# Shifting the SBUF addresses of a decoder trunk's matmul operands by 64 bytes, and ten more matmuls on zeros at the start

## The chip, the core and the metric

The kernel runs on one core of a Trainium2 chip. A core has TensorE (matrix products; PE in the profile, with its weight loads shown as PEld), VectorE (DVE), ScalarE (ACT), GpSimd (POOL) and SyncE (SP), which issues the DMA transfers. The engines work at the same time and wait for each other by semaphores. SBUF is the on-chip memory of 128 partitions from which TensorE reads both its operands; PSUM takes its results. The metric is the device time of one execution in microseconds.

## The reference

The computation is a decoder trunk of two layers on 256 tokens of width 1024, in float32. What matters of it:

```python
for l in range(DEPTH):                         # DEPTH = 2
    h = _rmsnorm(x, mix_norm[l])
    proj = h @ w_in[l]                         # 1024 -> 5892 columns
    ret_c, fox_c, rwkv_c, gate_c = split(proj)
    y_ret, y_fox, y_rwkv = retention(ret_c), forgetting_attention(fox_c), rwkv7(rwkv_c)
    merged = sum(gate_b * (y_b @ p_b[l]) for the three branches b)
    x = x + merged @ w_out[l]
    h = _rmsnorm(x, ffn_norm[l])
    g, u = split(h @ w_gate_up[l])             # 1024 -> 2 x 2816
    x = x + (silu(g) * u) @ w_down[l]          # 2816 -> 1024
return x
```

## The kernel before

**Products in three parts.** Activations lie transposed: 128 channels on the partitions, 256 tokens along the row. Float32 precision is kept by splitting each operand into a rounded high part and the low rest, and by forming three products for each block of 128 x 128 weights (`mm3`, L281 to L289): high weights by high activations (L285), high weights by low activations (L288), low weights by high activations (L289). A weight block is the stationary operand, which a load puts into the array, and the 256 columns of an activation part are the streamed operand. Products whose result has the tokens on the partitions (`mm3n`, L429 to L434) swap the roles: the activation part is loaded and 256, 260 or 512 columns of a weight part are streamed.

**Weights in pieces.** `weights()` lists all weights in the order of use, in transfers of 1 MB or less into one of three buffers (`raw`). `_piece` (L251 to L270) takes eight blocks of 128 columns from such a buffer: ScalarE rounds them into a tile `whi` (L268), VectorE subtracts and writes the rest into a tile `wlo` (L269). There are four buffers of each, in turn, and `refill` makes pieces up to three ahead of their use. One piece of eight blocks gives TensorE 24 matmuls of `mm3`. A pair of result blocks over 1024 channels takes two pieces (`gemm_pair`, L291), over 2816 channels five and a half.

**Stages of a layer.** (1) The mixers: products with the input weights, whose streamed operands are the tiles `xh` and `xl` made by `norm_add` (L379); among them, in an order that a table of paces (`PACE`) sets, the three branches with their many small matmuls; then twelve products of the branches' outputs (`hi`, `lo` in the pool `t2`), merged with the gates, and four output products (`hi`, `lo` in `t2` again). (2) The feed-forward part (`ffn`, L571): 22 pairs of gate and up products on `xh`, `xl`, and four pairs of down products on the hidden parts `hh`, `hl` (named `hi`, `lo` in the profile, in the pool `hp`). After the third pair, `replicate` (L421) spreads the norm's factors by one float32 matmul (L424). Within the feed-forward part, TensorE has nothing else to do than `mm3`.

**Where the tiles lie.** Pools are laid one after the other in SBUF, the tags of a pool in order of first use, and a pool that is opened inside a `with` takes the room behind those that are open. `cp`, `raw`, `spl` (the parts of the weights), `xp` (activations) are open throughout; `big`, `t2` and `sm` in the mixers; `hp` and `ft` in the feed-forward part. The addresses of the built program, per partition:

| tiles | address of the first, bytes | step from buffer to buffer | modulo 128 |
|---|---|---|---|
| `whi`, four buffers | 46784 | 4160 (1040 columns of 4 bytes) | 64, 0, 64, 0 |
| `wlo`, four buffers | 63424 | 4160 | 64, 0, 64, 0 |
| `xh` and `xl`, four each | 92352, 100544 | 2048 | 64 |
| `hh`, `hl` (feed-forward) | 113408 | 2048 | 0 |
| `hi`, `lo` of the branches and of the merge | 193376 | 2048 | 96 |

A block is 512 bytes and a half of an activation tile 1024, so the modulus holds within a tile. The two parts of a piece always lie in buffers of the same modulus. The buffers are taken in falling order of address: 0, 64, 0, 64 modulo 128.

**The start.** `__init__` (L152) clears a tile `zero` and runs 20 matmuls on it (L169, L170) into a PSUM tile that nobody reads, and issues the first transfers. Order and waits between engines are made by a planner from the program's order, the paces and priorities. `early` (L243) raises the priority of some work.

Of the kernel before, what the change touches and what calls it, by code (L numbers as in the profile page):

```python
# [8 lines left out]
F32 = mybir.dt.float32  # L9
F32R = mybir.dt.float32r  # L10
# [6 lines left out]
P = 128  # L17
# [133 lines left out]
class Kernel:  # L151
    def __init__(self, ctx, tc, d, depth=DEPTH, debug=None):  # L152
        self.tc, self.nc, self.d, self.depth = tc, tc.nc, d, depth
        self.debug = debug or {}
        nc = self.nc
        e = ctx.enter_context
        self.cp = e(tc.tile_pool(name="cp", bufs=1))
        self.raw = e(tc.tile_pool(name="raw", bufs=3))
        self.spl = e(tc.tile_pool(name="spl", bufs=4))
        self.xp = e(tc.tile_pool(name="xp", bufs=4))  # L160
        self.ps = e(tc.tile_pool(name="ps", bufs=4, space=bass.MemoryType.PSUM))
        self.dr = e(tc.tile_pool(name="dr", bufs=1, space=bass.MemoryType.DRAM))
        self.uid = 0


        zero = self.cp.tile([P, T], mybir.dt.bfloat16, name="zero")
        nc.vector.memset(zero, 0.0)
        pz = self.ps.tile([P, T], F32, tag="fr", bufs=2, name="pz")
        for _ in range(20):  # L169
            nc.tensor.matmul(pz, zero[:, 0:P], zero, start=True, stop=True)  # L170
        par = [self.cp.tile([P, P_RES], F32, name=f"par{l}") for l in range(depth)]
        self.xt = [self.xp.tile([P, 2, T], F32, tag="x", bufs=5, name=f"x0_{j}") for j in range(4)]
        nc.sync.dma_start(self.xt[0], d["xt"][:, 0:2, :])
        nc.sync.dma_start(par[0], d["par"][0, :, 0:P_RES])
        self.jobs, self.raws, self.ready, self.cur = list(self.weights()), [], [], []
        w0 = self.raw.tile([P, 2080], F32, tag="raw", name=self.nm("raw"))
        for j in range(4):
            if j:
                nc.sync.dma_start(self.xt[j], d["xt"][:, 2 * j:2 * j + 2, :])
            if j < 2:  # L180
                nc.sync.dma_start(w0[:, 1024 * j:1024 * (j + 1)], d["win"][0, 0, :, 1024 * j:1024 * (j + 1)])
        self.jobs[0:1] = [(w0, 4, P, 0), (w0, 4, P, 4), (w0, 8, P, 8)]
        self.par = par
        self.con = con = self.cp.tile([P, C_RES], F32, name="con")
        self.identb, self.maskb = zero[:, 0:P], zero[:, P:]
        self.c = {}
        for k, (o, n) in C_OFF.items():
            if k in FETCHED:
                continue
            v = con[:, o:o + n]  # L190
            if k in C_SHAPE:
                v = v.rearrange("p (a b) -> p a b", a=C_SHAPE[k][0])
            self.c[k] = v
        cc = self.c["cc"]
        self.cc = lambda i: cc[:, i:i + 1]

    def load_rest(self):
        self.nc.sync.dma_start(self.con, self.d["const"][:, 0:C_RES])
        self.nc.gpsimd.tensor_copy(self.identb, self.c["ident"])
        self.nc.gpsimd.tensor_copy(self.maskb, self.c["foxmask"])  # L200
        for l in range(1, self.depth):
            self.nc.sync.dma_start(self.par[l], self.d["par"][l, :, 0:P_RES])
# [48 lines left out]
    def _piece(self):  # L251

        nc = self.nc
        if not self.raws:
            src, n, width, o = self.jobs.pop(0)
            if hasattr(src, "shape") and src.shape[-1] == n * width:
                raw = self.raw.tile([P, 2080], F32, tag="raw", name=self.nm("raw"))
                nc.sync.dma_start(raw[:, :n * width], src)
            else:
                raw = src  # L260
            per = min(8, 1040 // width)
            for s in range(0, n, per):
                self.raws.append((raw, o + s, min(per, n - s), width))
        raw, s, m, width = self.raws.pop(0)
        r = raw[:, s * width:(s + m) * width]
        hi = self.spl.tile([P, 1040], F32R, tag="whi", name=self.nm("whi"))
        lo = self.spl.tile([P, 1040], F32R, tag="wlo", name=self.nm("wlo"))
        nc.scalar.copy(hi[:, :m * width], r)  # L268
        nc.vector.tensor_tensor(out=lo[:, :m * width], in0=r, in1=hi[:, :m * width].bitcast(F32), op=ALU.subtract)  # L269
        self.ready.append([(hi[:, i * width:(i + 1) * width], lo[:, i * width:(i + 1) * width]) for i in range(m)])  # L270
# [187 lines left out]
    def layer(self, l):  # L458
        tc, nc, d = self.tc, self.nc, self.d
        if l == 0:  # L460
            self.norm_start(0, "mixg")
            for j in range(4):
                self.norm_add(j, False)
                if j != 2:
                    self.piece()
        xs = self.xs
        with ExitStack() as st:
            e = st.enter_context
            self.big = e(tc.tile_pool(name="big", bufs=1))
            self.t2 = e(tc.tile_pool(name="t2", bufs=13))  # L470
            self.sm = e(tc.tile_pool(name="sm", bufs=1))
            self.mixers(l, xs)
            mx = self.mx

            self.norm_start(l, "ffng")
            for j in range(4):
                if j == 0:
                    ps = self.gemm_halves(mx, 4)
                elif j == 3:
                    ps = self.gemm_halves(mx)  # L480
                else:
                    ps = self.run(self.gemm_pair(mx))
                x = self.xp.tile([P, 2, T], F32, tag="x", bufs=5, name=self.nm("x"))
                for o, p in self.parts(ps):
                    nc.vector.scalar_tensor_tensor(out=x[:, o, :], in0=p, scalar=0.5, in1=self.xt[j][:, o, :], op0=ALU.mult, op1=ALU.add)
                self.xt[j] = x
                self.norm_add(j)
        self.ffn(l)
# [82 lines left out]
    def ffn(self, l):  # L571
# [3 lines left out]
        with ExitStack() as st:  # L575
            e = st.enter_context
            hp = e(tc.tile_pool(name="hp", bufs=1))
            ft = e(tc.tile_pool(name="ft", bufs=3))
            for j in range(FT // 2):
                if j == 0:  # L580
                    pg = self.gemm_halves(xs, 7, tag="rw")
                    _, dg = self.rstd()
# [11 lines left out]
                hi, lo = self.split(hp, h, [P, 2, T], (f"hh{j}", f"hl{j}"))  # L594
# [595 lines left out]
```

## Time and profile before

| | |
|---|---|
| time, median of 3 runs | 813.24 us (812.84 to 814.67) |
| the profiled execution: its own time | 813.39 us |
| its span, first to last instruction | 811.5 us |
| mean granted TensorE clock | 0.995 |
| PE busy, share of the span | 797.3 us, 98% |
| DVE, ACT, POOL busy | 575.2, 397.0, 62.9 us |

A row of the view by windows has the stretch (us from the span's start), its length, then for each engine the busy time and the number of instructions that ran in it, the granted TensorE clock, the busy share of the DMA engines and GB/s. An instruction that began before the stretch and ends in it counts too: a matmul's record is 0.28 us long while the next one begins some 0.11 us after it, so 26 or 27 in a row mean 24 that begin there. A row of the timeline has the start, the duration, engine, line, operation, result<-operands, shapes and how many are merged.

### The profile page before, as it was taken

Reading aid. Unit: us, or ns where it says so; the run is one execution under the profiler, and the core shown is the slowest. Engines: PE = TensorE matmul, PEld = TensorE weight load, DVE = VectorE, ACT = ScalarE, POOL = GpSimd, SP = SyncE. Lnnn points to the kernel's source line nnn. Section 1 sums busy time; section 2 is a strip of 40 time slices with the busy share of each in tenths; the row PEclk is TensorE's granted clock in tenths of the full one; section 3 lists DMA queues with packets and bytes.
Section 4 is the critical chain, followed back from the end, with each engine's and each line's share of the span. In section 5 each row is a group of like instructions: output and inputs, shape, how many; then the busy total and the mean of one; then the engine's idle time right before and its main releaser. Section 6 shows DMA issues by size and latency. Waiting matters only on the chain.

```text
span 811.5 us, 16511 instructions
## 1 busy us (share of the span) xinstructions
PE 797.3 (98%) x7008; PEld 777.1 (96%) x7008; DVE 575.2 (71%) x900; ACT 397.0 (49%) x543; POOL 62.9 (8%) x78
## 2 busy tenths in 40 slices
PE   8999899999999999999999999999999999999998
PEld 7999899999999999999998998999999999999997
DVE  6897978597867656646668788877877766666453
ACT  6367445435645445444444763544455544444331
POOL 3111210021000000000022021001010000000000
PEclk8999999999999999999999999999999999999999
DMA  8564524335454555555554552553445455554650
GB/s 310 195 224 168 164 94 161 129 126 187 163 201 166 199 197 170 191 172 202 201 177 174 210 170 105 164 166 105 156 157 208 156 208 186 180 206 159 204 184 27
DMA packets 27802, 140.42 MB, mean 173 GB/s; under 512 B 7600, under 2 KB 9168, under 8 KB 12496
## 3 DMA queue, kind: packets, MB, share of 16 engines
q1 hardware_dynamic: 27728, 139.36, 49.6%
q8 instruction: 55, 0.90, 0.5%
q14 instruction: 19, 0.16, 0.1%
HBM read 136.97 MB, written 1.33 MB: 170 GB/s over the span
## 4 chain that ended last, share of the span: by engine, by line
PE 92%; DVE 4%; DMA 2%; POOL 1%; issue 1%; ACT 0%; SPq 0%; POOLq 0%; ACTq 0%
PE mm L285 27%; PE mm L289 27%; PE mm L288 26%; DVE wlo L269 1%; DMA x<-in_xt 1%; PE mqk L433 1%; PE mqk L434 1%; PE mqk L432 1%; DMA rsw<-rqk 1%; PE pgm L755 1%; PE mv L432 1%; PE mv L434 1%; PE mv L433 1%; PE ptr L790 0%; DVE rkk L738 0%
## 5 line engine op out<-in xcount | busy, mean ns | idle before, releaser
L268 ACT CAST whi<-raw 128x1024 fp32r<-128x1024 f32 (+1 forms) x257 | 264.4, 1032 | 336.6 <-PE mm L288 244.0
L269 DVE TENSOR_TENSOR wlo<-raw,whi 128x1024 fp32r<-128x1024 f32 (+1 forms) x257 | 314.2, 1225 | 146.2 <-ACT whi L268 145.3
L285 PE MATMUL mm<-xh,whi 128*128 128x256 f32 x1312 | 372.2, 284 | 2.2 <-ACT whi L268 1.9
L288 PE MATMUL mm<-xl,whi 128*128 128x256 f32 x1248 | 349.6, 280 | 0.0
L289 PE MATMUL mm<-xh,wlo 128*128 128x256 f32 x1248 | 349.2, 280 | 0.0
L285 PEld LDWEIGHTS mm<-xh,whi 128*128 128x128 f32 x1312 | 249.1, 190 | 4.7 <-ACT whi L268 2.2
L288 PEld LDWEIGHTS mm<-xl,whi 128*128 128x128 f32 x1248 | 235.8, 189 | 0.8 <-issue 0.5
L289 PEld LDWEIGHTS mm<-xh,wlo 128*128 128x128 f32 x1248 | 235.9, 189 | 0.2
L285 PE MATMUL mm<-hi,whi 128*128 128x256 f32 x576 | 161.7, 282 | 0.0
L289 PE MATMUL mm<-hi,wlo 128*128 128x256 f32 x544 | 152.6, 280 | 0.0
L288 PE MATMUL mm<-lo,whi 128*128 128x256 f32 x544 | 152.5, 280 | 0.0
L285 PEld LDWEIGHTS mm<-hi,whi 128*128 128x128 f32 x576 | 108.7, 189 | 0.6 <-issue 0.3
L289 PEld LDWEIGHTS mm<-hi,wlo 128*128 128x128 f32 x544 | 102.7, 189 | 0.2
L288 PEld LDWEIGHTS mm<-lo,whi 128*128 128x128 f32 x544 | 102.6, 189 | 0.1
L593 DVE TENSOR_TENSOR h<-t,mm 128x512 f32<-128x512 f32 x22 | 15.1, 687 | 14.5 <-PE mm L289 11.6
L563 POOL TENSOR_TENSOR gate<-gate,gate 128x512 f32<-128x512 f32 x10 | 13.3, 1336 | 143.8 <-DVE gate L561 143.8
L590 DVE TENSOR_TENSOR t<-mm,rstd 128x512 f32<-128x512 f32 (+1 forms) x24 | 15.1, 644 | 10.9 <-PE mm L289 10.9
L561 DVE SCALAR_TENSOR_TENSOR gate<-gate,mm 128x512 f32<-128x512 f32 x24 | 16.2, 683 | 8.9 <-PE mm L289 8.7
L547 DVE TENSOR_TENSOR gate<-mm,rstd 128x512 f32<-128x512 f32 x24 | 16.5, 688 | 4.7 <-PE mm L289 4.3
L288 PE MATMUL mm<-xh,wlo 128*128 128x256 f32 x64 | 19.1, 301 | 0.3 <-DVE wlo L269 0.3
L289 PE MATMUL mm<-xl,whi 128*128 128x256 f32 x64 | 19.2, 303 | 0.0
L434 PE MATMUL mv<-whi,xl 128*128 128x260 f32 (+1 forms) x64 | 18.6, 290 | 0.0
(258 smaller groups left out, 796.0 us busy)
## 6 DMA issues: line engine op xcount, KB each, us to landing
raw<-in_wg SPq DMA_DIRECT2D x44, 1024.0 KB, 4.8
raw<-in_wgate SPq DMA_DIRECT2D x24, 1024.0 KB, 5.0
raw<-in_wd SPq DMA_DIRECT2D x16, 1024.0 KB, 5.0
raw<-in_win SPq DMA_DIRECT2D x13, 1024.0 KB, 8.2
raw<-in_wo SPq DMA_DIRECT2D x8, 1024.0 KB, 4.7
raw<-in_pp SPq DMA_DIRECT2D x6, 1024.0 KB
raw<-in_wd SPq DMA_DIRECT2D x8, 768.0 KB, 4.3
raw<-in_wqk SPq DMA_DIRECT2D x4, 1024.0 KB, 4.9
```

Of the source, the lines that this page charges most:

```text
L268: nc.scalar.copy(hi[:, :m * width], r)
L269: nc.vector.tensor_tensor(out=lo[:, :m * width], in0=r, in1=hi[:, :m * width].bitcast(F32), op=ALU.subtract)
L285: nc.tensor.matmul(out, wh, xh, start=first, stop=False)
L288: nc.tensor.matmul(out, wh, xl, start=False, stop=False)
L289: nc.tensor.matmul(out, wl, xh, start=False, stop=last)
L432: nc.tensor.matmul(out, xh[:, s], wh, start=first, stop=False)
L433: nc.tensor.matmul(out, xh[:, s], wl, start=False, stop=False)
L434: nc.tensor.matmul(out, xl[:, s], wh, start=False, stop=last)
L547: nc.vector.tensor_tensor(out=g, in0=ps, in1=self.b2(rstd), op=ALU.mult)
L561: nc.vector.scalar_tensor_tensor(out=g, in0=g, scalar=1.0, in1=ps, op0=ALU.add, op1=ALU.mult)
L590: nc.vector.tensor_tensor(out=t[:, o, :], in0=p, in1=self.bs(rstd, o), op=ALU.mult)
L593: nc.vector.tensor_tensor(out=h, in0=t, in1=pu, op=ALU.mult)
```

## The change

The tiles `whi` and `wlo` become 1056 columns long, of which the same 1040 at most are written and read: a buffer then takes 4224 bytes, 33 times 128. A new method `pad` allocates a small tile at the head of a pool and clears it on GpSimd, which moves all that lies behind it: by 16 columns (64 bytes) in `xp`, 24 (96 bytes) in `big`, once a layer, and 16 in `hp`, once a layer. And 30 matmuls on zeros take the place of 20.

```diff
-        for _ in range(20):
+        for _ in range(30):
             nc.tensor.matmul(pz, zero[:, 0:P], zero, start=True, stop=True)
         par = [self.cp.tile([P, P_RES], F32, name=f"par{l}") for l in range(depth)]
+
+        self.pad(self.xp, 16)
         self.xt = [self.xp.tile([P, 2, T], F32, tag="x", bufs=5, name=f"x0_{j}") for j in range(4)]
...
+    def pad(self, pool, n):
+        self.nc.gpsimd.memset(pool.tile([P, n], F32, tag="pad", bufs=1, name=self.nm("pad")), 0.0)
...
-        hi = self.spl.tile([P, 1040], F32R, tag="whi", name=self.nm("whi"))
-        lo = self.spl.tile([P, 1040], F32R, tag="wlo", name=self.nm("wlo"))
+        hi = self.spl.tile([P, 1056], F32R, tag="whi", name=self.nm("whi"))
+        lo = self.spl.tile([P, 1056], F32R, tag="wlo", name=self.nm("wlo"))
...
             self.big = e(tc.tile_pool(name="big", bufs=1))
+            self.pad(self.big, 24)
             self.t2 = e(tc.tile_pool(name="t2", bufs=13))
...
             hp = e(tc.tile_pool(name="hp", bufs=1))
+            self.pad(hp, 16)
             ft = e(tc.tile_pool(name="ft", bufs=3))
```

Worked out from the sizes, the addresses are then:

| tiles | address of the first, bytes | modulo 128 |
|---|---|---|
| `whi`, four buffers, step 4224 | 46784 | 64 in all |
| `wlo`, four buffers, step 4224 | 63680 | 64 in all |
| `xh`, `xl` | 92928, 101120 | 0 |
| `hh`, `hl` | 114048 | 0 |
| `hi`, `lo` of the branches and of the merge | 194048 | 0 |

From one weight buffer to the next the address still moves by 128 modulo 256. The tiles of `big`, `t2` and `sm` all move by the same 672 bytes.

## The prediction

> **What bounds the kernel now.** I read the page first: the engines' busy times, the granted clock in slices, and the chain of work that ended last.
>
> ```profile
> span 811.5 us, 16511 instructions
> PE 797.3 (98%) x7008; PEld 777.1 (96%) x7008; DVE 575.2 (71%) x900; ACT 397.0 (49%) x543; POOL 62.9 (8%) x78
> PEclk8999999999999999999999999999999999999999
> PE 92%; DVE 4%; DMA 2%; POOL 1%; issue 1%; ACT 0%; SPq 0%; POOLq 0%; ACTq 0%
> PE mm L285 27%; PE mm L289 27%; PE mm L288 26%; DVE wlo L269 1%; DMA x<-in_xt 1%; PE mqk L433 1%; PE mqk L434 1%; PE mqk L432 1%; DMA rsw<-rqk 1%; PE pgm L755 1%; PE mv L432 1%; PE mv L434 1%; PE mv L433 1%; PE ptr L790 0%; DVE rkk L738 0%
> ```
>
> TensorE is on the chain for 92%, and the three lines of the split product alone are 27 + 26 + 27 = 80% of the span. The clock is full after the first slice. So the time is a number of matmuls times the step from one to the next, and a change that touches addresses can only matter through that step. A busy TensorE is no proof that the step is the shortest one, so I then cut the time where the weight buffer changes (every 24 matmuls, seen by address in the built program) and read the length of each such stay in the view by windows.
>
> ```profile
> core 0: us, PE busy (x), PEclk, DMA share, GB/s
> 298.26:300.99 2.73, 2.73 (x26) 1.00 0.39 162
> 300.99:303.87 2.88, 2.88 (x26) 1.00 0.68 228
> 303.87:306.60 2.73, 2.73 (x27) 1.00 0.38 153
> 306.60:309.44 2.84, 2.84 (x27) 1.00 0.72 205
> ...
> 366.86:369.59 2.73, 2.73 (x27) 1.00 0.64 189
> 369.59:372.42 2.83, 2.83 (x26) 1.00 0.71 223
> 372.42:375.16 2.74, 2.74 (x26) 1.00 0.66 251
> 375.16:378.04 2.88, 2.88 (x26) 1.00 0.00 0
> 135.12:137.95 2.83, 2.83 (x27) 1.00 0.93 355
> 213.20:216.03 2.83, 2.83 (x26) 1.00 0.79 316
> 216.03:218.83 2.80, 2.80 (x26) 1.00 0.75 249
> 218.83:221.71 2.88, 2.88 (x27) 1.00 0.35 148
> 221.71:224.52 2.81, 2.81 (x26) 1.00 0.73 239
> ```
>
> The first four rows are gate and up products, with `xh` and `xl` at 64 modulo 128, on the buffers at 0, 64, 0, 64: 2.73, 2.88, 2.73, 2.84. The next four are down products, with `hh` and `hl` at 0, on buffers at 64, 0, 64, 0: 2.73, 2.83, 2.74, 2.88. The buffer that was slow at 300.99 is the very one that is fast at 366.86, and the one at 298.26 is that of 375.16. So neither the buffer nor the stage sets the length. Loaded and streamed operand **together** in the modulus cost 2.83 to 2.88, **apart** by 64 they cost 2.73: 120 against 113.6 ns a matmul at the ends. The last four rows, merge products with operands at 96, lie 32 from either kind of buffer: 2.81 to 2.88. The row at 135.12 is apart, too, and yet takes 2.83; it is the base of my main rival.
>
> **The change part by part: the layout.** After it every load of a weight part is at 64 and every streamed operand of `mm3` at 0, so all stays are apart. What a steady stay takes is the row of one that begins and ends in the fast rhythm, and how many there are stands in the rows of matmuls that write the products' tiles, in four stretches cut at L424 and at a wait:
>
> ```profile
> 303.99:306.71 2.72, 2.72 (x26) 1.00 0.33 133
> 17.29:242.38 225.09, 166.18 (x1347) 1.00 0.48 166
> 242.38:422.07 179.69, 179.49 (x1538) 1.00 0.54 186
> 422.07:639.55 217.48, 160.27 (x1298) 1.00 0.47 162
> 639.55:811.50 171.95, 168.00 (x1440) 1.00 0.49 167
> ```
>
> A round of four stays is 2.73 + 2.88 + 2.73 + 2.84 = 11.18 us, and 2.73 + 2.83 + 2.74 + 2.88 = 11.18 in the down products. All apart it is 4 x 2.72 = 10.88, so 0.30 less. The second stretch has 1536 matmuls (1538 less the two that began before), 64 stays, 16 rounds: 4.8 us. The fourth has 1440, 60 stays, 15 rounds: 4.5. In both TensorE fills the stretch (179.69 of 179.69 busy, below), so all of it is on the chain: **9.3 us**.
>
> The first and third stretch, the mixers, have 1344 and 1296 matmuls of this kind, 56 and 54 stays, of which 14 each use operands at 96 (twelve merge products of 12 matmuls and four output products of 48, 336 together). At best those 14 go from 2.83 + 2.80 + 2.88 + 2.81 = 11.32 a round to 10.88, 3.5 rounds x 0.44 = 1.5, and the others, 42 and 40, give 10.5 and 10 rounds x 0.30 = 3.2 and 3.0: 9.2 us together. At worst all settle at the 2.83 of the row at 135.12: a round is then 11.32, no gain for the 28 and a loss of 20.5 rounds x 0.14 = 2.9. The mixers break off often, for small matmuls and waits, and after each break the rhythm is chosen anew, so I take a value between, a little above the middle of 3.2 because part of the apart stays there are slow today: **4.0 us**. That it reaches the end is the case if nobody else is the limit:
>
> ```profile
> 17.29:242.38 225.09, 221.30 (x2009) 212.23 (x2008) 182.39 (x333) 114.90 (x172) 26.28 (x26) 1.00 0.48 166
> 242.38:422.07 179.69, 179.69 (x1543) 179.69 (x1541) 110.25 (x123) 85.89 (x103) 4.22 (x11) 1.00 0.54 186
> ```
>
> (after the length: PE, PEld, DVE, ACT, POOL.) In the feed-forward part VectorE works 110 of 180 us and makes the weights in time; in the mixers it works 182 of 225, and TensorE idles 3.8.
>
> The loads' own rule speaks against all this. The Trainium skill ("TensorE: Matmul & The Clock Gate", "Step-by-step: what each phase is for") says that TensorE reads the operand to be loaded and the streamed one by two independent ports, so that loading the next weights takes nothing from the running matmul. By it every stay would last the same and the layout would be worth 0. The rows disagree: 2.73 and 2.88 with the same count, engine and clock. As a rival it stands below.
>
> **The other layout effects.** The 288 products with swapped roles (L432 to L434) stream weight parts that start 0 to 112 past the modulus, before as after; by the 0.16 us / 24 = 6.7 ns that a step can differ, their bound is 288 x 6.7 ns = 1.9 us either way, and I take 0. The small matmuls read tiles of `big` and `t2` against each other, which move by the same 672 bytes: 0. The writes of `whi` and `wlo` keep their 1040 columns: 0. The pads are five clears on POOL, each priced by the first row here, queued ahead of nothing that is due: POOL works 63 of 811 us. Without that cover they would cost 5 x 0.14 = 0.7. One of them, in the second layer, waits for the hidden parts below it to be read, and behind it wait only clears of tiles in the same room.
>
> **30 matmuls on zeros.**
>
> ```profile
> 0.73 0.14 POOL L633 MEMSET pj<- 128x2 f32 x2 [0.29 <-POOLq L1178]
> 1.05 4.33 PE L170 MATMUL pz<-zero 128*128 128x256 bf16 x20 [1.05 <-DVE zero L167]
> 7.25 0.38 PE L285 MATMUL mm<-xh,whi 128*128 128x256 f32 x1 [1.87 <-ACT whi L268]
> 15.17 2.45 DVE L269 TENSOR_TENSOR wlo<-raw,whi 128x1024 fp32r<-128x1024 f32 x2 [0.24 <-ACT whi L268]
> 17.53 0.28 PE L289 MATMUL mm<-xh,wlo 128*128 128x256 f32 x1
> 5.38:8.55 3.17, 0.96 (x6) 1.00 0.99 317
> 8.55:15.37 6.82, 6.48 (x30) 0.50 1.03 417
> ```
>
> The twenty end at 5.38, and the first product starts at 7.25, when ScalarE has the weights. Ten more take 10 x 4.33 / 20 = 2.2 us at the half clock, to 7.5, or half of it, so they delay the first product by 0.3 at most, while it needs data that come later anyway. What they can win is the half clock from 8.55 to 15.37, which follows the pause. If it stays full, the second product is limited by its low weights, ready at 15.17 + 2.45 / 2 = 16.4 and now used at 17.53: 1.1 at best. If the half clock only comes later, on a stretch where all data are there, 6.8 us hold 30 matmuls where 3.4 would do: 3.4 lost. I take **0.3** gained, near the best end, since most of the start waits for data under either clock.
>
> **Sum.** The profiled execution took 813.39 (median of the runs 813.24, no difference that matters). 813.39 - 9.3 - 4.0 - 0.3 = **799.8 us**. With the mixers' bounds it lies between 794.6 (9.2) and 806.7 (-2.9).
>
> **Rivals.** (1) *The slower rhythm stays, and it gets slower.* Apart allows two rhythms: 2.72, and the 2.83 at 135.12. The feed-forward part is entered like this:
>
> ```profile
> 241.84 0.59 PE L424 MATMUL pss<-dg,con 128*128 128x256 f32 x2
> 242.08 0.47 PE L285 MATMUL mm<-xh,whi 128*128 128x256 f32 x1
> 242.38 0.28 PE L288 MATMUL mm<-xl,whi 128*128 128x256 f32 x1
> 245.09 0.28 PE L285 MATMUL mm<-xh,whi 128*128 128x256 f32 x1
> ```
>
> From 242.38 to 245.09 there are 23 steps of 117.8 ns: the slower rhythm, on a buffer apart. Today the next stay is together and the one after it runs at 2.73. After the change no stay together breaks it, and TensorE never pauses until 422. If the slower rhythm survives the shift by 128 bytes at the next buffer, it survives all of them, and 31 rounds of 11.32 for 11.18 lose 4.3. With the mixers then worth 0 (between 4.0 gained and 2.9 lost) the time is 813.39 + 4.3 - 0.3 = **817.4**, 813 to 820. For it: that entry; against it: the fast rhythm, once there, lasts, so one kick at any of 60 changes of buffer ends the slower one, and the entry comes after other addresses than before. It decides at the first change of buffer after L424.
> (2) *Only one of the two feed-forward stretches gets the fast rhythm.* The second one kept in the slower costs 4.8 + 16 x 0.14 = 7.0 beside the sum: **806.8**. The two layers run the same code, which speaks against it.
> (3) *The layout does nothing* and the rows differ for another cause: 813.39 - 0.3 = **813.1**. Against it is the exchange of fast and slow between the two kinds of products.
> (4) *VectorE becomes the limit in the mixers*, and the 4.0 go into waits for `wlo`: **803.8**. For it, 182 of 225 us; against it, TensorE's 3.8 us of idle time.
>
> **How the numbers follow.** Forecast 57%, (1) 20%, (2) 12%, (3) 5%, (4) 6%. A change of under 0.2% (1.6 us) can't be told from none here. Faster are the forecast, (2), (4) and a little of (1): 76%. Within 0.2% are (3) and the lower end of (1): 9%. Slower is the rest of (1): 15%. The range is 794 to 814: it holds the forecast between its bounds, (2), (3) and (4), and the lower end of (1). Cases of one sign hold most of the chance.
>
> **What would show it.** Right: four stays in a row of 2.72 in gate and up products and of 2.72 in down products; the stretch from L424 of the first layer to the wait in the second 4.8 us shorter than 179.69; merge products at 2.72 to 2.83 where they were 2.88 at most. Rival (1): row after row of 2.83. Rival (4): idle time before L288 and L289 put down to `wlo`. The clock at 8.55 to 15.37 tells the zeros' part. The forecast is wrong if a stay apart can take a third length, above 2.83.

## The result and the profile after

The changed kernel takes 800.01 us (median of four runs, 799.38 to 800.76) against 813.24 (four runs too, 812.84 to 814.67) before: a ratio of 0.9835, 95% interval 0.9818 to 0.9852. The forecast was 799.8. The profiled execution took 800.76, its span is 799.0, where that of before was 811.5, so 12.5 us are to be found.

In the new file the lines of the split product are L290, L293 and L294 (L285, L288, L289 before), those of the weight parts L273 and L274, the norm's factors are spread at L429, and L377, L748 and L1068 are the old L372, L741 and L1061. The page of the kernel after, its span, engines, clock by slices and chain:

```profile
span 799.0 us, 16543 instructions
...
PE 783.6 (98%) x7018; PEld 762.5 (95%) x7018; DVE 576.2 (72%) x900; ACT 397.1 (50%) x543; POOL 61.6 (8%) x83
...
PEclk9999999999999999999999999999999999999999
...
PE 88%; DVE 6%; DMA 2%; ACT 1%; issue 1%; POOL 1%; SPq 0%; POOLq 0%; DVEq 0%; ACTq 0%
PE mm L290 26%; PE mm L294 25%; PE mm L293 25%; DVE wlo L274 2%; PE mqk L439 1%; PE mqk L438 1%; PE mqk L437 1%; ACT whi L273 1%; DMA rsw<-rqk 1%; PE pgm L762 1%; DVE rkk L745 1%; DMA raw<-in_win 1%; DMA raw<-in_pp 1%; PE mv L437 1%; PE mv L439 1%
```

TensorE has ten matmuls more than before and is busy 13.7 us less: the step from one matmul to the next became shorter on average. The three product lines went from 80% of the chain to 76%, VectorE's share from 4 to 6%; the clock's first slice is full now. To see where the time was saved I cut both traces at the first product behind each run of L424 or L429 (the gates' products of the mixers, then gate and up). The view by windows, after the length PE, PEld, DVE, ACT, POOL; first the kernel after, then the kernel before:

```profile
0.00:28.32 28.32, 25.14 (x180) 22.20 (x181) 18.51 (x38) 16.09 (x24) 6.14 (x23) 1.00 0.82 287
28.32:238.70 210.38, 206.35 (x1906) 197.47 (x1905) 173.14 (x312) 109.30 (x167) 25.94 (x26) 1.00 0.47 165
238.70:420.04 181.34, 181.34 (x1592) 181.29 (x1591) 114.95 (x138) 88.11 (x105) 4.30 (x12) 1.00 0.55 193
420.04:630.92 210.88, 206.63 (x1906) 197.64 (x1905) 172.96 (x310) 110.46 (x168) 25.25 (x22) 1.00 0.46 161
630.92:799.00 168.08, 164.09 (x1442) 163.86 (x1440) 96.61 (x103) 73.16 (x83) 0.00 (x0) 1.00 0.50 172
```

```profile
0.00:29.17 29.17, 25.57 (x171) 23.32 (x171) 18.67 (x38) 16.29 (x24) 7.85 (x21) 0.88 0.78 277
29.17:242.08 212.91, 209.12 (x1907) 200.10 (x1905) 173.22 (x312) 109.28 (x167) 25.79 (x25) 1.00 0.47 163
242.08:427.76 185.68, 185.68 (x1593) 185.62 (x1591) 114.86 (x138) 88.02 (x105) 4.22 (x11) 1.00 0.54 188
427.76:639.24 211.48, 208.66 (x1906) 199.94 (x1905) 171.86 (x310) 110.33 (x168) 25.04 (x21) 1.00 0.47 160
639.24:811.50 172.26, 168.31 (x1442) 168.09 (x1440) 96.61 (x103) 73.09 (x83) 0.00 (x0) 1.00 0.49 168
```

The start became 0.85 shorter, the two mixers 2.53 and 0.60, the two feed-forward stages 4.34 and 4.18; together 12.5. The feed-forward stages are 68% of it, and in the first of them TensorE is busy for the whole stage in both kernels, so there the step itself is the time. The stays in the kernel after, by windows; four gate and up products, two down products, then the entry behind L429 and the change from `x` to the hidden values:

```profile
298.90:301.62 2.72, 2.72 (x26) 2.72 (x26) 2.14 (x3) 1.57 (x2) 0.00 (x0) 1.00 0.44 178
301.62:304.34 2.72, 2.72 (x26) 2.72 (x26) 1.60 (x2) 1.05 (x1) 0.00 (x0) 1.00 0.62 205
304.34:307.06 2.72, 2.72 (x26) 2.72 (x26) 1.92 (x2) 1.58 (x2) 0.00 (x0) 1.00 0.43 181
307.06:309.78 2.72, 2.72 (x26) 2.72 (x26) 1.23 (x1) 1.05 (x1) 0.00 (x0) 1.00 0.57 196
372.66:375.38 2.72, 2.72 (x26) 2.72 (x26) 2.72 (x3) 1.06 (x1) 0.00 (x0) 1.00 0.86 340
375.38:378.10 2.72, 2.72 (x26) 2.72 (x26) 2.20 (x4) 2.38 (x4) 0.00 (x0) 1.00 0.55 154
...
238.70:241.72 3.02, 3.02 (x27) 2.99 (x25) 2.10 (x4) 1.29 (x3) 0.00 (x0) 1.00 0.23 98
241.72:244.54 2.82, 2.82 (x26) 2.82 (x25) 1.13 (x3) 2.81 (x4) 0.00 (x0) 1.00 0.86 314
244.54:247.26 2.72, 2.72 (x26) 2.72 (x25) 2.72 (x4) 2.22 (x4) 0.00 (x0) 1.00 0.18 66
...
342.46:345.29 2.83, 2.83 (x26) 2.83 (x25) 2.29 (x3) 1.57 (x2) 0.00 (x0) 1.00 0.43 177
...
348.12:350.95 2.83, 2.83 (x27) 2.83 (x25) 0.69 (x1) 0.62 (x1) 0.00 (x0) 1.00 0.56 164
350.95:353.67 2.72, 2.72 (x27) 2.72 (x25) 1.22 (x1) 1.05 (x1) 0.00 (x0) 1.00 0.66 260
```

Where rows of 2.73 and 2.88 took turns before, the rows are now 2.72, in gate and up as in the down products. Merge products, which took 2.80 to 2.88, show 2.72 too (three stays in a row from 207.88). Two places differ: behind L429 the slower rhythm of rival (1) is there (2.82, and 3.02 with the gap of 0.3 at the entry), goes on over the first change of buffer and ends at the second; and it returns for three stays where the streamed operand changes from `xh` to `hh`, and for two shorter ones, from 402.6 to 407.6, where it changes back.

### The profile page after: what moved, and what is told of

The parts are those of the page before. It is cut to its first block, busy times and chain, and to the rows that moved or that the text cites. A ratio compares the mean times of both kernels' runs of the same rounds, so it can differ in the third digit from the quotient of the medians.

```text
span 799.0 us, 16543 instructions
## 1 busy us (share of the span) xinstructions
PE 783.6 (98%) x7018; PEld 762.5 (95%) x7018; DVE 576.2 (72%) x900; ACT 397.1 (50%) x543; POOL 61.6 (8%) x83
## 4 chain that ended last, share of the span: by engine, by line
PE 88%; DVE 6%; DMA 2%; ACT 1%; issue 1%; POOL 1%; SPq 0%; POOLq 0%; DVEq 0%; ACTq 0%
PE mm L290 26%; PE mm L294 25%; PE mm L293 25%; DVE wlo L274 2%; PE mqk L439 1%; PE mqk L438 1%; PE mqk L437 1%; ACT whi L273 1%; DMA rsw<-rqk 1%; PE pgm L762 1%; DVE rkk L745 1%; DMA raw<-in_win 1%; DMA raw<-in_pp 1%; PE mv L437 1%; PE mv L439 1%
## 5 line engine op out<-in xcount | busy, mean ns | idle before, releaser
L273 ACT CAST whi<-raw 128x1024 fp32r<-128x1024 f32 (+1 forms) x257 | 264.7, 1033 | 321.7 <-PE mm L293 232.2
L274 DVE TENSOR_TENSOR wlo<-raw,whi 128x1024 fp32r<-128x1024 f32 (+1 forms) x257 | 313.3, 1221 | 143.0 <-ACT whi L273 142.3
L290 PE MATMUL mm<-xh,whi 128*128 128x256 f32 x1312 | 368.0, 280 | 0.5 <-ACT whi L273 0.5
L294 PE MATMUL mm<-xh,wlo 128*128 128x256 f32 x1248 | 346.3, 277 | 0.7 <-DVE wlo L274 0.7
L293 PE MATMUL mm<-xl,whi 128*128 128x256 f32 x1248 | 346.3, 278 | 0.0
L290 PEld LDWEIGHTS mm<-xh,whi 128*128 128x128 f32 x1312 | 246.6, 188 | 2.8 <-issue 0.9
L294 PEld LDWEIGHTS mm<-xh,wlo 128*128 128x128 f32 x1248 | 234.4, 188 | 1.1 <-DVE wlo L274 0.9
L293 PEld LDWEIGHTS mm<-xl,whi 128*128 128x128 f32 x1248 | 234.5, 188 | 0.8 <-issue 0.5
L290 PE MATMUL mm<-hi,whi 128*128 128x256 f32 x576 | 160.1, 279 | 0.0
L294 PE MATMUL mm<-hi,wlo 128*128 128x256 f32 x544 | 150.9, 277 | 0.0
L293 PE MATMUL mm<-lo,whi 128*128 128x256 f32 x544 | 150.8, 277 | 0.0
L290 PEld LDWEIGHTS mm<-hi,whi 128*128 128x128 f32 x576 | 108.2, 188 | 0.6 <-issue 0.3
L294 PEld LDWEIGHTS mm<-hi,wlo 128*128 128x128 f32 x544 | 102.1, 188 | 0.2
L293 PEld LDWEIGHTS mm<-lo,whi 128*128 128x128 f32 x544 | 102.1, 188 | 0.1
L293 PE MATMUL mm<-xh,wlo 128*128 128x256 f32 x64 | 18.0, 281 | 0.7 <-DVE wlo L274 0.7
L437 PE MATMUL mv<-whi,xh 128*128 128x260 f32 (+1 forms) x64 | 18.6, 290 | 0.0
```

What stands on the lines that cost most here:

```text
L290: nc.tensor.matmul(out, wh, xh, start=first, stop=False)
L293: nc.tensor.matmul(out, wh, xl, start=False, stop=False)
L294: nc.tensor.matmul(out, wl, xh, start=False, stop=last)
L437: nc.tensor.matmul(out, xh[:, s], wh, start=first, stop=False)
```

## The experiments

The theory from here on: the step of a matmul hangs on the distance of the loaded and the streamed address modulo 128; a distance of 64 allows two rhythms, 113.3 and 117.8 ns, and what changes at the buffer decides which one lasts. Rivals: the layout is not the cause at all; each address counts by itself; the rhythm is chance. The stages of all kernels below, cut as above (us):

| kernel | median | mixers 1 | gate, up, down 1 | mixers 2 | gate, up, down 2 |
|---|---|---|---|---|---|
| before | 813.24 | 212.91 | 185.68 | 211.48 | 172.26 |
| after | 800.01 | 210.38 | 181.34 | 210.88 | 168.08 |
| e10_after, the same once more | 799.16 | 210.30 | 181.34 | 209.44 | 168.10 |
| e1_zeros, zeros alone | 813.1 | 212.54 | 185.68 | 212.52 | 172.25 |
| e2_layout, layout alone | 801.62 | 210.87 | 181.34 | 208.89 | 168.02 |
| e3_parts, longer parts alone | 818.29 | 214.03 | 186.65 | 214.01 | 172.83 |
| e4_minus | 817.02 | 213.35 | 187.43 | 211.95 | 173.89 |
| e5_plus | 802.63 | 209.87 | 182.98 | 209.89 | 169.89 |
| e7_same256 | 798.96 | 210.05 | 180.82 | 210.88 | 167.72 |
| e9_always64 | 798.68 | 209.87 | 180.63 | 209.93 | 167.55 |
| e11_turned | 799.31 | 210.48 | 180.94 | 211.31 | 167.84 |

The first feed-forward stage is the same to 0.01 us in each execution of a layout (185.68 twice, 181.34 three times), so there a difference of 0.1 can be read; the mixers vary by 1 to 2 us between executions.

### The step alone, by address (e6_sweep)

```diff
+            cases = [(0, o) for o in range(0, 64, 4)] + [(16, o) for o in (0, 8, 16, 32)]
+            for r in range(2):
+                for i, (m, o) in enumerate(cases):
...
+                    nc.tensor.matmul(ps, self.c["tri"][:, 0, P:], f, start=True, stop=True)
+                    for _ in range(40):
+                        nc.tensor.matmul(ps, wt[:, o:o + P], mv[:, m:m + T], start=True, stop=True)
```

> The changed kernel with work added behind its last product, which leaves its result as it is: 20 cases, run through twice, each of one fp32 matmul on zeros (it breaks off whatever rhythm there was) and 40 matmuls of one fp32r shape (128 columns loaded, 256 streamed). Only the addresses differ: streamed operand and loaded operand start 0, 16, 32, ... 240 bytes apart modulo 256 (cases a to p), and in the last four (q to t) the streamed operand is moved by 64 bytes and the loaded one is 0, 32, 64 or 128 bytes past the earlier one. Theory (the step hangs on the difference of the two addresses modulo 128, and the layout is the cause): 120.0 ns a step at differences 0 and 128, 113.3 or 117.8 at 64 and 192, in between 116.7 to 120; moving both operands together changes nothing. Rival A (the step hangs on each address by itself, a bank that an operand starts in): q to t follow the loaded operand's own address, not the difference. Rival B (something else in the kernel makes the difference, the layout does nothing): all cases show one step. Which of the two rhythms an apart case takes can't be told ahead; the two passes show whether it is chance. The time itself is about 185 us above the changed kernel's, for the added work.

The timeline of TensorE, one row for the 40 matmuls of a case (start, duration, result<-operands); distances 0, 64, 128 and 192, then the pairs moved together, at distance 192 and 0:

```profile
796.96 5.13 PE L218 MATMUL sua<-mv,wt 128*128 128x256 f32 x40
...
817.64 4.91 PE L218 MATMUL sue<-mv,wt 128*128 128x256 f32 x40
...
838.24 5.10 PE L218 MATMUL sui<-mv,wt 128*128 128x256 f32 x40
...
859.03 5.06 PE L218 MATMUL sum<-mv,wt 128*128 128x256 f32 x40
...
879.55 4.89 PE L218 MATMUL suq<-mv,wt 128*128 128x256 f32 x40
...
889.66 5.13 PE L218 MATMUL sus<-mv,wt 128*128 128x256 f32 x40
```

Nothing but addresses differs, and the same 40 matmuls take 5.13 or 4.89. From start to start the last twenty steps are 120.0 ns at distance 0 (`sua`, and `sus` with both moved by 64), 118.7 at 128, 113.3 or 117.8 at 64 and 192, and 116.7 to 120.0 at the twelve distances between. That ends the rival that addresses make no difference to the step. The Trainium skill ("TensorE: Matmul & The Clock Gate", "Step-by-step: what each phase is for") has two independent read ports for the two operands; by that all rows would be equal, and the measurement decides against it for these shapes. The rival of each address by itself falls for the together case (`sua` and `sus` lie differently and are both at 120.0), but the theory is not whole either. The distance counts modulo 256 and not 128: 0 and 128 differ, 16 and 144 are at 118.2 and 120.0, 80 and 208 at 118.9 and 116.7. And `sum` and `suq` have the same distance, 192, and are at 117.8 and 113.3, as the two cases at 64 are at 113.3 and 117.8. Both passes gave the same step in each of the 20 cases, within 0.1 ns.

### The two parts of the change apart (e1_zeros, e2_layout)

e1_zeros is the kernel before with this edit alone, e2_layout the changed kernel without it:

```diff
-        for _ in range(20):
+        for _ in range(30):
```

> The kernel before with 30 matmuls on zeros in place of 20 and nothing else. In the changed kernel the clock is full from 6.62 us on and the loading of the second layer's or first mixers' products begins 0.84 us earlier (28.32 against 29.17). Theory: that start is the zeros' alone and nothing later gives it back: 813.24 - 0.8 = 812.4 us, with a full clock from about 7 us on. Rival A (the prediction's own term): 0.3 gained, 812.9. Rival B (the start is not on the path, a later wait takes it): 813.2, with the first product after the mixers' first wait as early as in the changed kernel and the end where it was.

> The changed kernel with 20 matmuls on zeros in place of 30: the layout alone. Theory (the layout gives 12.4, the zeros 0.8, and they add up): 800.01 + 0.8 = 800.8 us, with the half clock from about 8.5 to 15.4 us as in the kernel before. Rival (the clock stays full in the start because of the layout or by chance, not by the zeros): 800.0 with a full clock in the start.

e1_zeros took 813.1 (812.21 to 814.34), ratio 0.9994, interval 0.9985 to 1.0003: 0.3, 0.8 and no gain at all lie in it. e2_layout took 801.62 (799.61 to 803.26), ratio 0.9856, 0.9841 to 0.9871. So the layout is the change, and the zeros are too small for the times. What they do is seen at the start; windows of the changed kernel, then of e2_layout:

```profile
8.55:15.37 6.82, 6.16 (x46) 5.56 (x47) 5.68 (x12) 5.47 (x11) 0.62 (x2) 1.00 1.02 412
```

```profile
8.55:13.12 4.57, 4.47 (x20) 4.34 (x21) 4.39 (x10) 4.11 (x9) 0.00 (x0) 1.00 1.03 414
13.13:15.37 2.24, 2.24 (x21) 2.24 (x21) 1.54 (x3) 1.36 (x2) 0.27 (x1) 1.00 1.03 431
```

With 20 zeros, 20 matmuls take 4.57 us and the next 21 take 2.24. The first row has steps of 0.21 us, half the speed, although its clock column reads 1.00; before, that column read 0.50 and 30 matmuls took 6.82. With 30 zeros, 46 fit into the 6.82 us. Thirty zeros do not always keep the clock full: of ten profiles with them, e6_sweep shows 0.50 in the column from 11.60 to 15.01, and 16 matmuls in these 3.41 us. The first mixers begin at 28.03 to 28.83 in these ten profiles, mean 28.44, and at 29.17, 28.58 (e2_layout) and 28.78 (e3_parts) with 20, mean 28.84: 0.4 us are left. Between 8.55 and the first mixers TensorE idles 1.32 us in the changed kernel, for `wlo` (1.0) and `xl` (0.3), and 0.34 us before; this takes back 1.0 of the 1.8 us that 16 matmuls are worth.

### Half of the layout (e3_parts)

The kernel before with

```diff
-        hi = self.spl.tile([P, 1040], F32R, tag="whi", name=self.nm("whi"))
-        lo = self.spl.tile([P, 1040], F32R, tag="wlo", name=self.nm("wlo"))
+        hi = self.spl.tile([P, 1056], F32R, tag="whi", name=self.nm("whi"))
+        lo = self.spl.tile([P, 1056], F32R, tag="wlo", name=self.nm("wlo"))
```

> The kernel before with one part of the change: the weights' parts 1056 columns long, so that all of them lie at 64 modulo 128, and no pads, so that xh and xl stay at 64 and hh and hl at 0. Then every product of the mixers and of gate and up that streams xh or xl has both operands together, every down product has them apart. Theory (together 2.88 us a stay, apart 2.72): a round of four stays in gate and up takes 11.52 in place of 11.18, one of down products 10.88; with some 20 stays rounds of the first kind a layer (+0.34 each at most, less in the mixers, where apart stays are partly slow) and some 5.5 of the second (-0.30) the sum is +4 to +10: 817 to 823 us, likeliest 820. Slower than before, with half of the change made. Rival A (any layout with all weights at one place modulo 128 is good, or longer parts themselves help): 800 to 807. Rival B (the layout does nothing): 813.

818.29 (817.47 to 818.82), ratio 1.0056, interval 1.0042 to 1.0069: slower, with half of a good change. Two neighbouring gate and up stays (PE alone):

```profile
303.07:305.95 2.88, 2.88 (x27) 1.00 0.78 239
305.95:308.79 2.84, 2.84 (x27) 1.00 0.33 136
```

Both are together modulo 128, the second with the operands 128 apart modulo 256, like the 118.7 of the sweep; all down stays are at 113.3. In the first feed-forward stage ten rounds cost 2 x (2.88 + 2.84) - 11.18 = 0.26 more each, 2.6, and 5.5 rounds of down products 0.30 less, 1.65: +0.95, and 186.65 - 185.68 = 0.97 was measured. The forecast's 0.34 a round had missed that 128 is not quite 0.

### All apart, without the alternation (e4_minus, e5_plus)

Both are the changed kernel with parts that put all weights at 192 modulo 256; e5_plus has the last edit as well:

```diff
-        hi = self.spl.tile([P, 1056], F32R, tag="whi", name=self.nm("whi"))
-        lo = self.spl.tile([P, 1056], F32R, tag="wlo", name=self.nm("wlo"))
+        hi = self.spl.tile([P, 1088], F32R, tag="whi", name=self.nm("whi"))
+        lo = self.spl.tile([P, 1088], F32R, tag="wlo", name=self.nm("wlo"))
...
-        self.pad(self.xp, 16)
+        self.pad(self.xp, 48)
```

> The changed kernel with the weights' parts 1088 columns long in place of 1056: all of them lie at 192 modulo 256, xh and xl stay at 0 and hh and hl at 128. Every product of a weight part loaded is still apart modulo 128, but the weights no longer alternate by 128 bytes from one buffer to the next (distance 192 for x, 64 for the hidden values, modulo 256). Theory (the alternation is what ends the slower rhythm of rival (1), which is entered behind the gates' products in front of gate and up): the slower rhythm, 117.8 ns a step, now lasts through gate and up, 40 stays x 0.107 us in each layer, perhaps through down too: 807 to 813 us. Rival (the fast rhythm is found anyway, at the first change of buffer or of product): 799 to 801.

> The mirror of the kernel e4_minus: parts of 1088 columns at 192 modulo 256, the pad in front of x 48 columns, so that xh and xl lie at 128 (distance 64 modulo 256) and hh and hl at 0 (distance 192). Theory: as there, without a change by 128 bytes the rhythm entered behind the gates' products lasts; if that is the slower one 807 to 813 us, if the sign of the distance decides which one is entered, one of the two kernels is at 807 to 813 and the other at 798 to 801. Rival (the fast rhythm is found anyway): both at 799 to 801.

e4_minus took 817.02 (815.71 to 818.25), ratio 1.0037, interval 1.0022 to 1.0051, although each product of a loaded weight part is apart modulo 128 exactly as in the changed kernel: 17 us slower than it. e5_plus took 802.63 (802.41 to 806.21), ratio 0.9872, 0.9850 to 0.9893. Windows of e4_minus (the stage, and a stay of it) and of e5_plus (the stage, a gate and up stay, a down stay):

```profile
241.92:429.35 187.43, 187.43 (x1592) 187.38 (x1591) 114.90 (x138) 88.03 (x105) 4.28 (x12) 1.00 0.54 186
299.99:302.82 2.83, 2.83 (x26) 2.83 (x26) 1.24 (x2) 1.41 (x2) 0.00 (x0) 1.00 0.26 41
```

```profile
238.04:421.02 182.98, 182.98 (x1592) 182.93 (x1591) 114.89 (x138) 88.08 (x105) 4.29 (x12) 1.00 0.55 191
298.69:301.41 2.72, 2.72 (x27) 2.72 (x26) 2.12 (x3) 1.58 (x3) 0.00 (x0) 1.00 0.19 72
...
372.69:375.52 2.83, 2.83 (x26) 2.83 (x25) 2.83 (x4) 1.06 (x1) 0.00 (x0) 1.00 0.80 327
```

In e4_minus the stage is entered in the slower rhythm and all its stays keep it, 2.83 each; that is rival (1). In e5_plus it is entered in the fast one, all of gate and up keep that, and the change from `x` to the hidden values sets the slower one on, which all down products keep, from 341.6 to 403.8. So without the alternation of the buffers a rhythm once there lasts until the streamed operand moves, and the rival that the fast one is found anyway is refuted. Neither time lies where it was expected (807 to 813, or 798 to 801): in e4_minus the slower rhythm holds the down products and the mixers as well, where only 95 and 3 of the 1248 matmuls of `mm` are followed by a step under 115.5 ns, and in e5_plus the down products have it.

### What changes the rhythm (e8_switch)

```diff
+            A, B, C, D, E, F = (0, 16), (0, 48), (16, 0), (16, 32), (32, 16), (32, 48)
+            cases = [(B, A, B, A), (D, C, D, C), (A, B, A, B), (C, D, C, D),
+                     (A, E, A, E), (B, F, B, F), ((0, 0), A, (0, 0), B), ((0, 0), B, (0, 32), A)]
...
+                    for m, o in seq:
+                        for _ in range(24):
+                            nc.tensor.matmul(ps, wt[:, o:o + P], mv[:, m:m + T], start=True, stop=True)
```

> The changed kernel with other work added behind its last product, its result as it is: eight cases, twice, each of one fp32 matmul on zeros and four stays of 24 matmuls (128 columns loaded, 256 streamed) with no pause between them. In cases a to d the streamed operand stays and the loaded one moves by 128 bytes from stay to stay (distance, loaded less streamed modulo 256: a 192, 64, 192, 64; b and c 64, 192, 64, 192; d 192, 64, 192, 64); in e and f the streamed one moves by 128 bytes and the loaded one stays; g and h go from together to apart. In the sweep, the first stay of a and b ran at 117.8 ns a step, that of c and d at 113.3. Theory, from the changed kernel's trace (there the slower rhythm ended at changes from 192 to 64 and began where the streamed operand moved by 128 bytes): case a gets fast in its second stay and stays so; b stays slow in its second and gets fast in its third; c and d stay fast throughout; e or f show fast stays turning slow; g and h, out of the together stay, come out in the one or the other rhythm, the same in both passes. Rival A (a rhythm once there is kept until a pause): a and b stay at 117.8 in all four stays, c to f keep the rhythm of their first. Rival B (the rhythm is chosen by chance at each change): the two passes differ.

Windows of e8_switch, PE alone: the four stays of case e, in which the streamed operand moves (distance 64, 192, 64, 192; the first stay has 0.2 of the entry in it):

```profile
840.04:842.97 2.93, 2.93 (x27) 1.00 0.00 0
842.97:845.79 2.82, 2.82 (x26) 1.00 0.00 0
845.79:848.52 2.73, 2.73 (x27) 1.00 0.02 6
848.52:851.34 2.82, 2.82 (x26) 1.00 0.00 0
```

By the steps of all 16 sequences: a move of the streamed operand by 128 bytes broke the fast rhythm 6 times of 6 (each time the move up by 32 columns, with the distance going from 64 to 192 or the other way; the moves back fell on stays that were slow already); a move of the loaded one broke it in none of 18. A slow rhythm ended at 8 of 9 changes of the distance from 192 to 64 and at none of 3 from 64 to 192. The expectation held for c, e, f, g, h and the first pass of a; in the second pass a got fast only in its fourth stay, and b and d entered the other rhythm than the same addresses did in the sweep. Rival A falls (a rhythm does change without a pause), rival B holds in one case of eight. So: what a change of address does is mostly regular, but which rhythm an entry gets isn't told by the addresses alone.

### Three better layouts and a repeat (e7_same256, e9_always64, e11_turned, e10_after)

e7_same256 is the changed kernel with the first edit here, e11_turned has both, and e9_always64 has both and the parts of 1088 columns; e10_after is the changed kernel.

```diff
-            self.pad(hp, 16)
+            self.pad(hp, 48)
...
-        self.pad(self.xp, 16)
+        self.pad(self.xp, 48)
```

> The changed kernel with the pad in front of the hidden values 48 columns in place of 16: hh and hl move from 128 to 0 modulo 256, where xh and xl are. In the changed kernel, three stays run at 117.8 ns a step at the change from x to the hidden values (342.5 to 350.9 us) and two at the change back (402.6 to 407.6). Theory (a streamed operand that moves by 128 bytes kicks the slower rhythm on): these five stays a layer run at 113.3, 5 x 0.107 = 0.5 us a layer, 1.1 us together: 799.0, the stage from the last gate product to the next layer's mixers 180.8 in place of 181.34. Rival (the slow stays come from the other products around the change, not from the address modulo 256): 800.0 and the five slow stays still there.

> The kernel e5_plus with the pad in front of the hidden values 48 columns in place of 16: now every product of a loaded weight part, with x, the merged and the hidden values alike, has the same distance, loaded less streamed 64 modulo 256, and no address moves by 128 bytes from one stay to the next. In e5_plus gate and up ran fast from the first stay (238.0 us) and the move to the hidden values set the slower rhythm on, which then lasted to 403.8. Theory (a rhythm lasts while the distance does, this entry is fast, and only the move kicks it): gate, up and down all at 113.3 ns, the stage from the last gate product 62 us x 4.5/117.8 = 2.4 us shorter than the 182.98 of e5_plus, 180.6, in the second layer 169.88 - 2.2 = 167.7; mixers as there, 209.9: 798.1 us in all. Rival (the rhythm of the entry is chance, and without the alternation nothing ends a slow one): one stage or both at 117.8, 187.4 or 174: 804 to 811.

> The kernel e7_same256 with x, merged and hidden values all moved by 128 bytes (pad in front of x 48 columns): the same alternation of the weights, but each distance 64 is now 192 and the other way round. In e7_same256 the two first stays behind the gates' products ran at 117.8 and the second change of buffer, 192 to 64, ended that. Theory (the slower rhythm ends at changes from 192 to 64): the first change is now of that kind, so one slow stay in place of two, 0.1 us a layer: 798.8. Rival (the end of the slower rhythm hangs on the time since the entry or on the buffer itself, not on the sign): again two slow stays, or another number, 799.0; a difference the times can't show, the stays can. If the entry is fast outright, neither.

> The changed kernel once more, beside the two kernels of this call on the same chip: 800.0 us by the theory that its time is set by addresses and not by the chip; its feed-forward stage 181.34 us again, and stay by stay the same rhythm. Rival (the rhythm there is chance): another length of that stage.

The stage, and the stay that was slow behind the change to the hidden values, in e7_same256; the stage in e9_always64:

```profile
238.09:418.91 180.82, 180.82 (x1592) 180.77 (x1591) 114.90 (x138) 88.12 (x105) 4.29 (x12) 1.00 0.55 193
341.85:344.57 2.72, 2.72 (x27) 2.72 (x25) 2.18 (x3) 1.57 (x2) 0.00 (x0) 1.00 0.44 184
```

```profile
238.29:418.92 180.63, 180.63 (x1593) 180.58 (x1591) 114.90 (x138) 88.08 (x105) 4.28 (x12) 1.00 0.56 193
```

With the hidden values where `x` is modulo 256, the five slow stays are gone and the stage is 0.52 shorter, as expected (180.8). With one distance for everything, nothing is slow in gate, up and down, and 180.63 and 167.55 came out where 180.6 and 167.7 were expected. The times are 798.96 (798.19 to 799.38) and 798.68 (798.20 to 799.68), where 799.0 and 798.1 were expected. The repeat of the changed kernel took 799.16 (798.65 to 800.60) beside the latter, with its feed-forward stage at 181.34 and the same stays slow there. The 1.2 us that e9_always64 saves in the two stages are plain in the trace; in the times they are not told from none, with ratios of 0.9822 (0.9808 to 0.9835) and 0.9832 (0.9818 to 0.9845). For e7_same256, too, it is the stays that decide, not the time.

e11_turned missed: three slow stays at the entry in place of the one expected. The first change from 192 to 64 did not end the slower rhythm, the second did, in both layers. So a change from 192 to 64 doesn't suffice for the end. It took 799.31 (799.04 to 800.68).

## Why the prediction was right, step by step

**The sum.** The forecast of 799.8 is 0.2 from the median of 800.01, and that closeness is luck: the terms add up to 13.6 us, where 12.5 were found in the profiled execution, which itself took 0.75 more than the median. Feed-forward and mixers were put 0.8 and 0.9 too high and the zeros 0.55 too low, while the four runs differ by 1.4. What was right is the mechanism and the size of each term to about 1 us.

**The bound.** That the time is a count of matmuls times a step, and that the step is shortest where the two addresses lie 64 apart modulo 128, was read from two rounds of four stays and holds: the sweep shows it with nothing else around, and the layout alone carries the gain. That the distance counts modulo 128 holds for this shortest step alone; elsewhere the sweep has it modulo 256 (120.0 at 0, 118.7 at 128).

**The feed-forward stretches: 9.3 forecast, 8.5 measured** (4.34 + 4.18). The step that was mis-sized is "all stays 2.72": 57 of the first stretch's 64 are, and about seven run at 2.83, two at the entry and five at the two changes of the streamed operand. (Two more stays, behind the stretch's end at L419, have the slower rhythm in every changed kernel.) Without any of them the two stages are 5.05 and 4.71 shorter than before (e9_always64), a little over the 4.8 and 4.5 worked out. That TensorE fills both stretches was misread for the second layer, where it is busy 168.00 of 171.95; but the rest lies behind the last product, in both kernels, and the 4.18 reached the end.

**The mixers: 4.0 forecast, 3.1 measured** (2.53 + 0.60), and 4.65 in the repeat (2.61 + 2.04), 4.6 with the layout alone (2.04 + 2.59). The value taken between far bounds was about right, which is partly luck, since nothing ahead of the change told how often the fast rhythm would be entered. By the steps from start to start, 704 and 690 of the 1248 matmuls of `mm` in the two mixers are followed by one under 115.5 ns, against 370 and 352 before; in the repeat it is 750 and 789. So close to half of them still take longer, and how many varies between executions. The split products themselves became shorter by more; the rows of their tiles, after and then before:

```profile
28.32:238.70 210.38, 151.69 (x1248) 146.01 (x1249) 24.13 (x38) 1.00 0.47 165
420.04:630.92 210.88, 151.77 (x1248) 146.10 (x1249) 24.11 (x38) 1.00 0.46 161
```

```profile
29.17:242.08 212.91, 154.28 (x1249) 148.53 (x1249) 24.18 (x38) 1.00 0.47 163
427.76:639.24 211.48, 154.35 (x1248) 148.60 (x1249) 24.18 (x38) 1.00 0.47 160
```

2.6 us each, 5.2 in all, of which 2.0 were given back. Most of this is idle time of TensorE: by the windows by stage it grew by 0.24 us in the first mixers (210.38 less 206.35, against 212.91 less 209.12) and by 1.43 in the second. TensorE's waits (in all, times, longest), after and then before, name where part of it went:

```profile
PE mm L294 <- POOL lo L377: 3.1, 2, 1.6
PE pb L748 <- DVE rkk L745: 2.9, 2, 1.5
PE px L1068 <- DVE lg L1064: 1.5, 2, 0.7
```

```profile
PE mm L289 <- POOL lo L372: 2.6, 2, 1.3
PE px L1061 <- DVE lg L1057: 2.0, 2, 1.3
...
PE pb L741 <- DVE rkk L738: 1.4, 1, 1.4
```

Products that end earlier wait longer for what VectorE and GpSimd make beside them: 1.5 more for `rkk`, 0.5 for `lo`, 0.5 less for `lg`. These waits move from execution to execution: the second mixers of the repeat have no wait for `rkk`, one of 1.5 for `lg` in place of 0.7, and last 209.44 in place of 210.88. So the waits account for 1.5 of the 2.0 and for part of the scatter; the rest stays open, and no run took one of them away.

**The zeros: 0.3 forecast,** 0.85 measured at the start of the one execution, 0.4 between the means of ten and three. The clock stayed full in the changed kernel, as the best end had it, though not in each profile with 30 zeros; and the wait for data took part of it back, as said.

**The other terms at nothing.** No run takes the products with swapped roles or the pads by themselves. They lie in the mixers and the start, whose scatter of 1 to 2 us would hide them.

**Rival (1)** was right in its mechanism and its price and wrong in where it decides. The slower rhythm was entered behind L429 as it said and did survive the first change of buffer, which the prediction had named as the point that decides. It ended at the second one. The reason that the prediction gave against it, that one kick at any change of buffer ends it, is what held, but only because the weights still alternate by 128 bytes. Where e4_minus takes that away the time is 817.02; the rival had said 817.4. That the two are so close is partly luck: its two feed-forward stages are 3.4 longer than before, not 4.3, and the mixers, put at 0, are 0.9 longer. **Rival (2)** did not happen: the feed-forward stays of both layers behave alike in every kernel. **Rival (3)** is refuted by the sweep and by e2_layout. **Rival (4)** is there in a small way: VectorE's share of the chain grew from 4 to 6%, with `wlo` from 1 to 2%. But in the mixers TensorE waits for `rkk` and never for `wlo`, which the rival had named; its waits for `wlo` lie in the start.

**What would have made it wrong** was a third length of an apart stay, above 2.83; none was seen in the feed-forward stages, the sweep or e8_switch.

## What to carry to other kernels

When a row of equal matmuls has unequal steps, compare the start addresses of the loaded and the streamed operand: in these runs 64 bytes apart modulo 128 was the only distance with the shortest step (113.3 ns), and the same place modulo 256 was among the longest (120.0, as at 112, 144 and 160). Put all streamed operands at one place modulo 256 and look at the stays again after a layout change, because a pair that is rightly apart can still sit in a slower rhythm for a whole stage. What is saved on TensorE must be followed into the stages where other engines feed it; there part of it came back as waits.

## What the runs showed of the hardware that was not expected

- One pair of addresses has two steady steps, 113.3 and 117.8 ns (case a of e8_switch has its first stay at 117.8 and its third, at the same addresses, at 113.3). Each of the two lasted for dozens of stays (e5_plus: gate and up in the one, down in the other). What chooses one at an entry stays open: the distance does not (64 is entered slow in the changed kernel and fast in e9_always64), and the same addresses entered different rhythms in e6_sweep and e8_switch. Yet it is not without weight: in the mixers, where many breaks make many entries, e4_minus (192) has 95 and 3 short steps of 1248, e5_plus and e9_always64 (64) 782 to 795.
- Moving the streamed operand by 128 bytes broke the fast rhythm each time in e8_switch and in the feed-forward stages, moving the loaded one never, though the step itself hangs on the distance of both. From one apart stay to the next, the slower rhythm ended there only where the distance went from 192 to 64 modulo 256, and not at each such change: not at 345.29 in the changed kernel, not at the first one in e11_turned, nor at the change to the down products in e4_minus.
- A stage of some 1500 matmuls in which TensorE never waits has the same length to 0.01 us in three executions (181.34). A busy TensorE and an equal time each run did not mean that nothing was left in it: the best layout took 180.63.
